# One fixed TensorE order from the inverse block to the first output tiles: attention as a generator of grouped steps

## The chip, the cores and the metric

One core of one Trainium2 chip runs the whole program. The metric is the device time of one execution in microseconds (us); before the change it is 1592.06 us, the median of 3 runs (1591.38 to 1592.39). PE is TensorE (matmuls), PEld its weight loads, DVE is VectorE, ACT is ScalarE, POOL is GpSimd, and SP is the engine that issues the DMA transfers.

## The reference

Two layers of a decoder trunk on a sequence of 512 tokens with 1024 channels, and a final norm. Cut to what matters here:

```python
n = RMSNorm(h);  p = n @ W_in                 # one input projection, split by columns
y_A = RWKV7_time_mix(p_A) @ W_oA              # 8 heads x 64, delta-rule state, group norm, gate
y_B = MLA(p_B) @ W_oB                         # 8 heads, causal softmax attention
h = h + (sigmoid(g_A) * y_A + sigmoid(g_B) * y_B) @ W_out
h = h + ConvFFN(RMSNorm(h))
...
# time mix, per token t and head
sa = state @ a_t
state = state * w_t + sa * b_t + v_t * k_t
y_t = state @ r_t
...
# attention, per block of 128 queries
s = (qn . kn + qr . kr) * scale;  s = where(causal, s, -1e30)
o = softmax(s) @ v
```

## The kernel before

**Products.** Activations lie with channels on the 128 partitions and the 512 tokens along the free axis. A weight product is done in split precision: `split` (L274) makes a high part `hi` on ACT and the remainder `lo` on DVE, and `mm3` (L245) does three matmuls of 128x512 per 128x128 weight block (L246 to L248). The weights stream from HBM in units of 512 KB (`raw`), which ACT and DVE split into `whi` (L201) and `wlo` (L202). `wtile` (L250) makes a tile of an output from 8 or 4 such blocks, and `Part` (L256) is the same piecemeal: `go(n)` does the next n blocks and, with the last, calls an end function.

**Order.** The program is written for a scheduler that puts every engine's instructions in an order of its own, by priority and readiness, except inside `manual_schedule`, where an engine keeps the order of the code. Every engine then works its queue strictly in that order, waiting on semaphores. Tiles come from pools with a number of buffers per tag: a tile that is asked for waits until the last reader of the one that had the buffer is done.

**A layer.** `mixer(l, ...)` (L425 to L962) begins with the input projection and the preparation of the time mix. Then, with TensorE in the order of the code (L647 to L815), come the triangular inverses of the chunks of 64 tokens, the rest of the projection (`parts4`: latents and gates), and the recurrence over 8 chunks c (L777 on): the state's read (L785), its sum xs (DVE, L789), the inverse applied (L795), a copy into Z (L798), the update's products with BT (L804), and the new state St (POOL and DVE, up to L815). Between these steps `filler()` puts two blocks of the gate products, six matmuls, as long as there are any left (`rest`).

What follows (L817 to L962) has no order of its own; the code comes as `outputs`, `norms`, `heads(0)`, `heads(1)`, `transposed`, `heads(2)`, `heads(3)` (L952), and the scheduler mixes it, and also pulls the products of the value tile Vt (L903) up into the recurrence:

- `chunk_out(i)` (L825): the chunk outputs into Z (copied by ACT, L844). `group_norm(i)` (L848) and `group_scale(i)` (L861): reductions on DVE, a square on ACT, a power (L858) and the scaling (L863) on POOL.
- `yop` (L867): four transposes of Z (L869) for a group p of 128 channels; loads of `bl` (L871) and `rg` (L873) from HBM, both with the tag "yl", which has two buffers; on DVE bl is scaled and summed (L874) and multiplied with rg (L875), then split, hi on ACT and lo on DVE (L279, L280). `transposed` does p = 0 and 1 in one PSUM tile xy, and then 2 and 3 in the next; there is one buffer for xy (two banks).
- `heads(p)` (L907), two heads at a time: the keys' products and K (ACT and POOL, L913), q (L921), and then, for each block b of 128 queries, a head at a time: scores `sc` of n = 128(b+1) keys (L929), the masked row minimum (DVE, L932), exp (ACT, L935), reciprocal (DVE, L936), scaling (ACT, L937), transposes of P into `pt` (L940; one bank), the copy PT (L942: on ACT for odd b, on DVE for even), and the value products into `po` (L947), of both heads into the two halves of the array. At the end po is split (L950).
- The output tiles of y_A: 8 times `wtile(yops)` (L957), four blocks each.

[...]

## Time and profile before

| what | us |
|---|---|
| median of 3 runs | 1592.06 |
| the profiled execution | 1593.16 |
| its span, first to last instruction | 1591.4 |
| TensorE busy | 1562.6 (98%) |
| DVE, ACT, POOL busy | 915.4, 661.5, 184.7 |
| inverse block to first output tile, layer 0 | 126.30 (227.60 to 353.90) |
| the same, layer 1 | 126.20 (1013.00 to 1139.20) |
| mean granted TensorE clock | 0.997 |

The span is 1.8 us shorter than the profiled execution's own time, which lies 1.1 us above the median. In the rows of a timeline the columns are the start, the duration, the engine, the line and operation, what it writes and reads, the shapes, and in brackets the idle time before it and what ended that. A row may hold several instructions of a kind (x4); a product in scores or values counts two records, a transpose or a matmul of a weight product one. A row of waits has the total, the number and the longest.

### The profile page before, as it was taken

The numbers are of one execution on the slowest core, as the hardware profiler recorded it, in microseconds if no ns is written. First come the engines' busy times: TensorE is split into PE (matmuls) and PEld (weight loads), VectorE is DVE, ScalarE is ACT, GpSimd is POOL, SyncE is SP. The second block draws the span as 40 slices with busy tenths as digits, with TensorE's granted clock in tenths as the row PEclk, the third lists the DMA queues.
The fourth block names the chain that finished last, engine by engine and source line by source line (L and its number), as shares of the span: only waits on it lengthen the run. The fifth ranks groups of instructions, "written<-read, shape, count | busy, mean of one in ns | idle before, by whom it ended". The sixth has DMA issues, their size and how long they took to land.

```text
span 1591.4 us, 22441 instructions
## 1 busy us (share of the span) xinstructions
PE 1562.6 (98%) x9052; PEld 1254.2 (79%) x9052; DVE 915.4 (58%) x1468; ACT 661.5 (42%) x996; POOL 184.7 (12%) x156
## 2 busy tenths in 40 slices
PE   8999999899999999999999999998999999999998
PEld 6878886668888888888878888775788888888887
DVE  6579786666555555533346668757564655554332
ACT  6445444563443333422244443446533434333222
POOL 1011102300311101100001111013002111010000
PEclk9999999999999999999999999999999999999999
DMA  5323322224423233233343233213253332332232
GB/s 192 125 100 132 121 81 67 88 74 147 123 96 99 93 97 102 93 108 120 110 146 106 94 106 120 74 48 101 86 162 103 97 102 93 95 104 93 93 104 82
DMA packets 57272, 166.08 MB, mean 104 GB/s; under 512 B 6352, under 2 KB 8528, under 8 KB 57168
## 3 DMA queue, kind: packets, MB, share of 16 engines
q1 hardware_dynamic: 57024, 164.48, 31.9%
q8 instruction: 71, 1.16, 0.3%
q14 instruction: 33, 0.27, 0.1%
q10 hardware_dynamic: 144, 0.16, 0.0%
HBM read 147.32 MB, written 17.30 MB: 103 GB/s over the span
## 4 chain that ended last, share of the span: by engine, by line
PE 91%; DVE 4%; issue 2%; ACT 1%; POOL 1%; DMA 0%; SPq 0%; POOLq 0%; DVEq 0%; ACTq 0%
PE acc L246 26%; PE acc L247 26%; PE acc L248 26%; PE sc L929 2%; PE po L947 2%; PE pt L940 1%; PE m L599 1%; PE xy L795 1%; DVE wlo L202 1%; PE m L607 1%; PE m L583 0%; PE xy L804 0%; PE m L524 0%; DVE X L661 0%; POOL mu L858 0%
## 5 line engine op out<-in xcount | busy, mean ns | idle before, releaser
L246 PE MATMUL acc<-hi,whi 128*128 128x512 f32 (+1 forms) x1910 | 752.4, 394 | 7.2 <-ACT hi L282 5.2
L248 PE MATMUL acc<-hi,wlo 128*128 128x512 f32 (+1 forms) x1910 | 742.6, 389 | 1.2 <-DVE wlo L202 1.2
L247 PE MATMUL acc<-lo,whi 128*128 128x512 f32 (+1 forms) x1910 | 742.8, 389 | 0.0
L201 ACT CAST whi<-raw 128x1024 fp32r<-128x1024 f32 (+2 forms) x249 | 253.5, 1019 | 547.2 <-PE acc L247 466.9
L246 PEld LDWEIGHTS acc<-hi,whi 128*128 128x128 f32 x1910 | 359.6, 188 | 82.5 <-ACT hi L282 5.2
L248 PEld LDWEIGHTS acc<-hi,wlo 128*128 128x128 f32 x1910 | 359.6, 188 | 76.1 <-DVE wlo L202 1.6
L247 PEld LDWEIGHTS acc<-lo,whi 128*128 128x128 f32 x1910 | 359.9, 188 | 72.4 <-issue 1.2
L202 DVE TENSOR_TENSOR wlo<-raw,whi 128x1024 fp32r<-128x1024 f32 (+2 forms) x249 | 309.5, 1244 | 175.9 <-ACT whi L201 175.5
L1027 POOL TENSOR_TENSOR c<-c,rstd 128x512 f32<-128x512 f32 x44 | 58.0, 1318 | 403.5 <-ACT c L1026 403.5
L1020 DVE TENSOR_TENSOR u<-acc,rstd 128x512 f32<-128x512 f32 x44 | 30.4, 692 | 104.7 <-PE acc L248 104.6
L1029 DVE TENSOR_TENSOR c<-c,acc 128x512 f32<-128x512 f32 x44 | 30.3, 688 | 86.4 <-POOL c L1027 86.4
L1026 ACT ACTIVATE c<-c 128x512 f32<-128x512 f32 x44 | 27.8, 632 | 81.6 <-DVE c L1025 81.6
L305 POOL TENSOR_TENSOR nv<-nv,cst 128x4 f32<-128x4 f32 (+1 forms) x10 | 10.0, 997 | 352.6 <-DVE nv L304 352.6
L341 POOL TENSOR_TENSOR nacc<-nacc,nsq 128x512 f32<-128x512 f32 x14 | 25.0, 1787 | 200.3 <-ACT nsq L340 200.3
L450 DVE TENSOR_TENSOR cur<-acc,rstd 128x512 f32<-128x512 f32 x28 | 19.1, 690 | 48.4 <-PE acc L248 39.3
L929 PE MATMUL sc<-K,q 128*128 128x128 f32 (+3 forms) x128 | 44.6, 446 | 1.1 <-DVE q L921 1.1
L935 ACT ACTIVATE P<-P,mn 128x128 f32<-128x128 f32 (+3 forms) x64 | 35.6, 556 | 17.2 <-issue 9.3
L932 DVE CUSTOM_DVE_ANT_0 P<-sc,cst 128x128 f32<-128x128 f32 (+3 forms) x64 | 30.7, 483 | 12.9 <-PE pt L940 10.4
L947 PE MATMUL po<-PT,Vt 128*64 128x128 f32 x320 | 37.5, 286 | 0.6 <-DVE PT L942 0.6
L937 ACT ACTIVATE P<-P,mn 128x128 f32<-128x128 f32 (+3 forms) x64 | 34.2, 557 | 6.6 <-DVE mn L936 6.6
L1023 ACT ACTIVATE c<-u,vec 128x512 f32<-128x512 f32 x44 | 35.7, 812 | 2.8 <-DVE u L1019 2.8
L947 PEld LDWEIGHTS po<-PT,Vt 128*64 128x64 f32 x320 | 22.3, 136 | 18.2 <-issue 7.3
(242 smaller groups left out, 1370.8 us busy)
## 6 DMA issues: line engine op xcount, KB each, us to landing
raw<-in_w SPq DMA_DIRECT2D x238, 512.0 KB, 3.4
gate_d<-gg SPq DMA_DIRECT2D x32, 256.0 KB, 2.1
AM<-gate_d SPq DMA_DIRECT2D x16, 256.0 KB, 5.9
gb<-gate_d SPq DMA_DIRECT2D x16, 256.0 KB, 3.6
h<-in_x SPq DMA_DIRECT2D x8, 256.0 KB, 4.6
rgate_d<-gt SPq DMA_DIRECT2D x8, 256.0 KB, 2.5
bl_d<-rk SPq DMA_DIRECT2D x8, 256.0 KB, 2.0
bl<-bl_d SPq DMA_DIRECT2D x8, 256.0 KB, 2.6
```

Of the source, the lines that this page charges most:

```text
L201: A.copy(hi, r)
L202: V.tensor_tensor(lo, r, hi.bitcast(F32), ALU.subtract)
L246: PE.matmul(ps, w[0], xx[0], start=first, stop=False)
L247: PE.matmul(ps, w[0], xx[1], start=False, stop=False)
L248: PE.matmul(ps, w[1], xx[0], start=False, stop=last)
L929: PE.matmul(sp[:, 0:n], qs[hh][:, 128 * b:128 * b + 128], ks[hh][:, 0:n], start=True, stop=True)
L932: V.tensor_tensor_reduce(out=P[:, 0:n], in0=sp[:, 0:n], in1=cst[:, C_CAUS + 512 - n:C_CAUS + 512], scale=-ATT_SCALE, scalar=1e30, op0=ALU. ...
L935: A.activation(P[:, 0:n], P[:, 0:n], AF.Exp, bias=mn[:, 0:1], scale=-1.0, accum_out=mn[:, 1:2])
L937: A.activation(P[:, 0:n], P[:, 0:n], AF.Copy, scale=mn[:, 2:3])
L947: PE.matmul(po[64 * hh:64 * hh + 64, 128 * b:128 * b + 128], Vt[:, kb, 64 * hd:64 * hd + 64], PTs[hh][:, 128 * kb:128 * kb + 128], start=k ...
L1023: A.activation(cc, u[:, 2:514], AF.Identity, bias=vc(l, "conv_b", i), scale=vc(l, "conv_w", 2 * FT + i))
L1027: G.tensor_tensor(cc, cc, rstd, ALU.mult)
```

## The change

TensorE's `manual_schedule` (an ExitStack `order`) now goes on from the inverse block through the recurrence, the attention, the chunk outputs, the transposes and the first four output tiles, so the order of all these on TensorE is that of the code; the other engines' order is still the scheduler's. Attention becomes a generator `attention(yops, ow)`: each `yield` ends a step of some matmuls, and `filler(n)` takes n steps of it wherever the recurrence and the chunk outputs leave room. A step t has the scores of both heads of one block, two or three pieces of `extra` (the next heads' projection, at the end the first output tiles), the transposes of the block before, head by head, and between them the value products of the block before that, both heads in pairs. The operations themselves are those of before.

Buffers: K and q together from 5 to 8, P and PT from 3 to 4 each, mn from 4 to 6. The gate parts' tile gg moves to a pool that lives longer (L711 after). The tags "yl" (2), sc, pt, po and xy are as before. A parameter of the program object, `dynamic_dma_scratch_size=1024`, is new. `heads`, `outputs`, `norms`, `transposed` and the old `filler` go.

```diff
+            order = ExitStack()
+            order.enter_context(tc.manual_schedule(engines={PE.engine}))
...
+                def attention(yops, ow):
+                    while parts4[7].i < 8:
+                        parts4[6 if parts4[6].i < 8 else 7].go(1)
+                        yield
...
+                            K = MT("K", "qk", 8)
...
+                    def turned(p, b, hh):
+                        n = 128 * (b + 1)
+                        pt = pb.tile([128, 512], F32, name="pt", tag="pt")
+                        for kb in range(b + 1):
+                            PE.transpose(pt[:, 128 * kb:128 * kb + 128], Ps[p, b][hh][:, 128 * kb:128 * kb + 128], ident)
+                        PT = MT("PT", "PT", 4)
+                        (A.copy if b % 2 else V.tensor_copy)(PT[:, 0:n], pt[:, 0:n])
+                        PTs.setdefault((p, b), []).append(PT)
...
+                    for t in range(18):
+                        if t < 16:
+                            p, b = steps[t]
+                            if b == 0:
+                                extra = project(p + 1) if p < 3 else ow()
+                            scores(p, b)
+                            yield
+                        for _ in range(2 if b < 3 else 3):
+                            if next(extra, 0) is None:
+                                yield
+                        if 0 < t < 17:
+                            turned(*steps[t - 1], 0)
+                        if t > 1:
+                            values(*steps[t - 2])
+                        if 0 < t < 17:
+                            yield
+                            turned(*steps[t - 1], 1)
+                        yield
...
                 for c in range(8):
...
-                        filler()
                         xs = tl.tile([128, 4, 2, 64], F32, name="xs", bufs=1)
...
+                        filler(2)
...
-                    filler()
                     V.tensor_copy(Z[ur:ur + 64, i, e, :].rearrange("p (q h i) -> p q h i", h=2, i=64),
                                   xy[ur:ur + 64, :, 256:512].rearrange("p h (q i) -> p q h i", i=64))
+                    filler(2)
...
-                        filler()
                         Sn = tl.tile([128, 4, 64], F32, name="St", tag="St", bufs=7)
...
+                        filler(1)
...
+                for i in range(4):
+                    chunk_out(i)
+                    filler(2)
+                grs = []
+                for i in range(4):
+                    grs.append(group_norm(i))
+                for i, gr in enumerate(grs):
+                    group_scale(i, gr)
+                filler(6)
+                for p in range(0, 4, 2):
+                    ps = xyt()
+                    yop(ps[:, 0, :], p)
+                    yop(ps[:, 1, :], p + 1)
+                    filler(2)
+                for _ in att:
+                    pass
+                while len(gas) < 4:
+                    firsts[len(gas)].go()
+                order.close()
+                for m in range(4, KT):
+                    ow_end(wtile(yops))
```

TensorE's order, first at two blocks of the attention in the middle of it, before (sc are scores, pt transposes of P, po value products, L246 to L248 weight products):

```order
L929 MATMUL sc<-K,q 128x384
L947 MATMUL po<-PT,Vt 64x128 x2
L940 MATMUL pt<-cst,P 128x128 x2
L247 MATMUL acc<-lo,whi 128x512
L929 MATMUL sc<-K,q 128x512
L940 MATMUL pt<-cst,P 128x128 x2
L947 MATMUL po<-PT,Vt 64x128
L929 MATMUL sc<-K,q 128x512
L947 MATMUL po<-PT,Vt 64x128 x3
L940 MATMUL pt<-cst,P 128x128 x3
```

The same on TensorE afterwards:

```order
L846 MATMUL pt<-cst,P 128x128 x2
L857 MATMUL po<-PT,Vt 64x128 x2
L846 MATMUL pt<-cst,P 128x128 x2
L828 MATMUL sc<-K,q 128x512 x2
L846 MATMUL pt<-cst,P 128x128 x3
L857 MATMUL po<-PT,Vt 64x128 x4
L846 MATMUL pt<-cst,P 128x128 x3
L828 MATMUL sc<-K,q 128x128 x2
```

The four value products of a block stood as one and three, with a score between; they stand together now, between the two heads' transposes of the next block, and the scores of both heads stand together.

TensorE at the transposes of Z (L869 before, L993 after). Before, each set of four (the first one's last row leads here) stood apart from the next:

```order
L869 MATMUL xy<-cst,Z 128x128
L929 MATMUL sc<-K,q 128x512 x2
L940 MATMUL pt<-cst,P 128x128 x2
L947 MATMUL po<-PT,Vt 64x128
L869 MATMUL xy<-cst,Z 128x128 x4
L947 MATMUL po<-PT,Vt 64x128 x3
L940 MATMUL pt<-cst,P 128x128 x6
L947 MATMUL po<-PT,Vt 64x128 x6
L940 MATMUL pt<-cst,P 128x128 x4
L246 MATMUL acc<-hi,whi 128x512
L247 MATMUL acc<-lo,whi 128x512
L869 MATMUL xy<-cst,Z 128x128 x4
```

Afterwards on TensorE:

```order
L846 MATMUL pt<-cst,P 128x128 x2
L993 MATMUL xy<-cst,Z 128x128 x8
L828 MATMUL sc<-K,q 128x512 x2
L846 MATMUL pt<-cst,P 128x128 x3
L857 MATMUL po<-PT,Vt 64x128 x4
L993 MATMUL xy<-cst,Z 128x128 x8
L846 MATMUL pt<-cst,P 128x128 x3
```

Two sets of four now follow each other, with one step of attention between the first two sets and the last two.

DVE at the same place (L874 and L998 read xy into bl, L875 and L999 multiply with rg, ISA is the masked minimum). Before, between the second bl's product and the third bl:

```order
L875 TENSOR_TENSOR bl<-bl,rg 128x512
L921 TENSOR_TENSOR q<-acc,rq 128x512
L932 ISA P,mn<-sc,cst 128x128
L932 ISA mn 128x1
L932 ISA P,mn<-sc,cst 128x128
L932 ISA mn 128x1
L280 TENSOR_TENSOR lo<-po,hi 128x512
L936 RECIPROCAL mn<-mn 128x1
L932 ISA P,mn<-sc,cst 128x256
L932 ISA mn 128x1
L874 SCALAR_TENSOR_TENSOR bl<-xy,vec,bl 128x512
```

Afterwards on DVE, from the second bl on:

```order
L998 SCALAR_TENSOR_TENSOR bl<-xy,vec,bl 128x512
L838 RECIPROCAL mn<-mn 128x1
L848 COPY PT<-pt 128x384
L999 TENSOR_TENSOR bl<-bl,rg 128x512
L838 RECIPROCAL mn<-mn 128x1
L998 SCALAR_TENSOR_TENSOR bl<-xy,vec,bl 128x512
L848 COPY PT<-pt 128x384
L834 ISA P,mn<-sc,cst 128x128
```

The second bl's product with rg and the third bl now follow each other with a reciprocal between, and the scores of the next block are reduced behind them.

## Prediction

> **What bounds the kernel now.** I read the page first, then the engines' busy time by stages, then TensorE's waits in the stage that the change touches, and last the timelines of that stage on each engine.

> ```profile
> span 1591.4 us, 22441 instructions
> ```

> The stretches below are the two stages that the change rewrites (from the inverse block to the first output tile, layer 0 and layer 1) and, between them, a stretch of plain weight products. The columns are the stretch, its length, the busy time of PE, PEld, DVE, ACT and POOL, the granted clock, the DMA share and GB/s.

> ```profile
> 227.60:353.90 126.30, 120.29 (x1328) 84.21 (x1328) 80.62 (x200) 72.25 (x158) 21.78 (x24) 1.00 0.24 75
> 400.00:1000.00 600.00, 598.83 (x2846) 491.13 (x2845) 327.40 (x440) 231.45 (x300) 69.61 (x51) 1.00 0.33 106
> 1013.00:1139.20 126.20, 119.68 (x1286) 83.37 (x1279) 79.85 (x200) 71.66 (x157) 21.79 (x24) 1.00 0.24 76
> ```

> TensorE bounds the kernel: outside these stages it stands for 1.2 us in 600. Inside them it shows 6.01 and 6.52 us idle, and no other engine is near its limit (DVE 64% of the stage, ACT 57%). So the order of the work can win two things only: TensorE's waits, and time in which it is busy at less than its rate. The waits of the first stage, by what ended them:

> ```profile
> PE xy L869 <- POOL Z L863: 1.2, 1, 1.2
> PE pt L940 <- DVE mn L936: 0.7, 1, 0.7
> PE xy L795 <- DVE xs L789: 0.7, 1, 0.7
> PE xy L833 <- ACT Z L844: 0.7, 2, 0.3
> PE xy L869 <- ACT Z L844: 0.6, 1, 0.6
> PE xy L785 <- DVE St L812: 0.6, 1, 0.6
> ```

> They are many and short; the longest is 1.2 us. What a wait really costs is more than the idle time shown, since the end of a matmul is modelled long. TensorE's timeline (start, duration, group) gives the factor:

> ```profile
> 309.07 0.55 PE L940 MATMUL pt<-cst,P 128*128 128x128 f32 x3
> 310.36 0.52 PE L940 MATMUL pt<-cst,P 128*128 128x128 f32 x3 [0.74 <-DVE mn L936]
> ...
> 312.33 0.66 PE L940 MATMUL pt<-cst,P 128*128 128x128 f32 x4
> 312.74 0.48 PE L246 MATMUL acc<-hi,whi 128*128 128x512 f32 x1
> ...
> 314.49 0.43 PE L947 MATMUL po<-PT,Vt 128*64 128x128 f32 x2
> 314.85 0.50 PE L246 MATMUL acc<-hi,whi 128*128 128x512 f32 x1
> 315.19 0.39 PE L247 MATMUL acc<-lo,whi 128*128 128x512 f32 x1
> 315.42 0.40 PE L248 MATMUL acc<-hi,wlo 128*128 128x512 f32 x1
> 315.75 1.09 PE L947 MATMUL po<-PT,Vt 128*64 128x128 f32 x14
> 316.76 0.71 PE L929 MATMUL sc<-K,q 128*128 128x128 f32 x4
> ```

> Four transposes that nothing holds up take 312.74 - 312.33 = 0.41, so the three at 309.07 could be followed at 309.38; the next start at 310.36. That is 0.98 lost where 0.74 is shown, 1.3 times. The stages therefore lose about 6.01 x 1.3 = 7.8 and 6.52 x 1.3 = 8.5 us, **8.15 a layer**.

> **What the change gives: grouping.** Every matmul of the stage is still done. But the value products of a block (two records each here) now stand together, both heads' in pairs, where before the first of them usually stood alone: the two records at 314.49 cost 314.85 - 314.49 = 0.36 and the fourteen at 315.75 cost 1.01. Seven products leave one half of the array empty once, so an eighth rides along free: the lone one's 0.36 is what grouping saves. By the instruction order 14 of a layer's 16 blocks are split so, and none afterwards: 14 x 0.36 = 5.0 us. Second, each visit to the half-array form slows its neighbours: the product at 314.85 takes 0.34 and the one at 315.42 takes 0.33, against 0.23 for the one between, so a visit costs 0.21 beside its own work. The order has 9 fewer visits a layer: 1.9 us. Grouping saves 5.0 + 1.9 = **6.9 a layer**, if nothing waits more than before.

> **What the change costs: waits.** If every stop went as well, the gain would be 15.05 a layer. So the question is how much TensorE stands in the new order, which it can't leave: before, whatever was ready stood at the front; now the next instruction is fixed.

> (a) The transposes of y. Before, the four sets of four stood far apart; now two and two, with one attention step between. The rows of before, on TensorE:

> ```profile
> 305.34 0.33 PE L869 MATMUL xy<-cst,Z 128*128 128x128 f32 x1
> 305.51 1.88 PE L929 MATMUL sc<-K,q 128*128 128x512 f32 x4
> 307.23 0.38 PE L940 MATMUL pt<-cst,P 128*128 128x128 f32 x2
> ...
> 307.90 0.66 PE L869 MATMUL xy<-cst,Z 128*128 128x128 f32 x4
> 308.49 0.65 PE L947 MATMUL po<-PT,Vt 128*64 128x128 f32 x6
> 309.07 0.55 PE L940 MATMUL pt<-cst,P 128*128 128x128 f32 x3
> ...
> 319.78 0.60 PE L869 MATMUL xy<-cst,Z 128*128 128x128 f32 x4
> ```

> What each set waits for is on DVE, ACT and the DMA queue. DVE:

> ```profile
> 305.75 0.75 DVE L874 SCALAR_TENSOR_TENSOR bl<-xy,vec,bl 128x512 f32<-128x512 f32 x1
> ...
> 306.53 0.69 DVE L875 TENSOR_TENSOR bl<-bl,rg 128x512 f32<-128x512 f32 x1
> ...
> 311.39 0.68 DVE L280 TENSOR_TENSOR lo<-bl,hi 128x512 fp32r<-128x512 f32 x1
> ...
> 314.71 0.69 DVE L875 TENSOR_TENSOR bl<-bl,rg 128x512 f32<-128x512 f32 x1 [1.32 <-DMA rg<-rgate_d]
> ```

> The loads, by time from issue to landing, and ACT, whose cast (L279) makes the high part:

> ```profile
> bl<-bl_d SPq DMA_DIRECT2D x8, 256.0 KB, 2.6
> rg<-rgate_d SPq DMA_DIRECT2D x8, 256.0 KB, 2.7
> ```
> ```profile
> 317.62 0.40 ACT L935 ACTIVATE P<-P,mn 128x128 f32<-128x128 f32 x1 [0.17 <-DVE mn L932]
> ...
> 318.02 0.60 ACT L279 CAST hi<-bl 128x512 fp32r<-128x512 f32 x1
> ...
> 320.24 0.80 ACT L937 ACTIVATE P<-P,mn 128x128 f32<-128x128 f32 x2
> ...
> 324.55 1.12 ACT L937 ACTIVATE P<-P,mn 128x384 f32<-128x384 f32 x2
> ```

> bl and rg have two buffers between them, and that is left as it was. So the second rg loads only when the first lo is done, and the third bl only when the second product with rg is. The last set shares its tile with the third and starts when DVE has read that one. From the end of the first set to the start of the fourth: 0.75 + 0.69 + 0.60 + 0.68 (first bl, product, hi, lo), 2.7 (rg lands), 0.69, 2.6 (bl lands), 0.75 = 9.5, and some 0.3 for seven handings-over (an estimate: 0.04 each, half of what lies between the modelled end of the transposes, 305.34 + 0.33, and DVE's read at 305.75): 9.8. TensorE has in that time two sets of transposes (0.41 to 0.59, from 307.90 to 308.49: 0.5 each), two scores of 512 (307.23 - 305.51 = 1.72), three transposes (0.4) and four value products (309.07 - 308.49 = 0.58) = 3.7. It stands for **6.1**: 0.8 before the second set, 0.9 before the third, which waits for the second bl, and 4.4 before the fourth. Before, the same chain took 319.78 - 305.34 = 14.4 with other work beneath and no stop, longer because lo came 4.2 us after its bl (311.39 against 307.22), behind softmax work on ACT and DVE. Were it 14.4 again, the stop would be 10.7; without the handings-over 5.8. I take 6.1, as hi and lo now directly follow their product on both queues.

> Queued behind those instructions are the copies of P's transposes (DVE) and the scaling of P (ACT), which TensorE wants next:

> (b) After the fourth set. ACT has two exp of 128 (0.40 each), hi of the second bl (0.60), two scales (0.80), two copies of K (0.60 each, as a 512-wide pass) and then the copy that frees the tile for transposed P (0.60), about 4.0 from when scores of 128 are reduced, 2 us into the stretch: 5.9. TensorE has two sets of transposes, two scores, six products of 0.23 to 0.34, four transposes and six value products, 4.3: a stop of 1.6. Then lo of the second bl, at 4.1, starts the buffer chain again: 2.7 + 0.69 + 0.60 + 0.68 + 2.7 + 0.69 + 0.60, and behind that last hi on ACT two scales of 384 (1.12) and a copy (0.40) = 14.3, where TensorE with its stop needs 11.7: a stop of 2.6. Together **4.2**; nothing, if ACT's and DVE's queues have run ahead while TensorE stood in (a).

> (c) The norms before the transposes. POOL carries the last part:

> ```profile
> 302.53 1.64 POOL L858 TENSOR_TENSOR mu<-mu,cst 128x8 f32<-128x8 f32 x1 [2.03 <-DVE mn L936]
> 304.24 1.04 POOL L863 TENSOR_TENSOR Z<-Z,mu 128x512 f32<-128x512 f32 x1
> ```

> For the last chunk: a copy (0.60), three DVE passes of 512 (0.69), a square on ACT (0.60), then 1.64 and 1.04 = 6.0, and DVE has among them a q, two P copies, two reductions of 384 and a lo, some 2.6, of which I count 2.1 on the path: 8.1. TensorE's cover after the chunk outputs is six products, three products, eight value products, two scores and six transposes, 5.2. Stop **2.9**; the ends are 1.2 (the shown wait on POOL alone) and 3.6.

> (d) The rest, inverse block and recurrence. The waits shown but for the two at L869 come to 6.0 - 1.8 = 4.2. Those on xs (0.7) and St (0.6) get products in front of them in every chunk and go: 2.9 x 1.3 = **3.8**. The state's cover falls from six products to three, 0.9 with the switch, against a wait of 0.6 x 1.3 = 0.8 where it had none: nothing, though it is thin. Ends: 2.5 (chunk outputs' 0.7 and one more go) and 5.5 (nothing goes).

> The larger buffers for K, q, P, PT and mn give the queues room to run ahead; they cost TensorE nothing, and with a fixed order they win only what (b) may lose.

> **The sum.** Stops 6.1 + 4.2 + 2.9 + 3.8 = 17.0 a layer against 8.15: +8.85. Grouping: -6.9. Net +1.95 a layer, +3.9 in two: span 1595.3. The profiled execution (1593.16, its span 1591.4) lies 1.1 above the median of the runs, 1592.06, so the forecast of the median is **1596.0**.

> **The rivals.** About 0.2%, 3.2 us, is what a measurement of this kernel can tell from no change. That is 1.6 a layer: with stops under 13.45 the change is faster, over 16.65 slower.

> Faster: while TensorE stands in (a), DVE and ACT finish all softmax work in hand, so (b) vanishes, (c) is the POOL wait of before (1.2) and (d) its low end. Stops 6.1 + 1.2 + 2.5 = 9.8; net -5.25 a layer: 1581.6. For it: DVE and ACT are idle for a third of the stage and more. Against it: the second chain in (b) is loads, which idle engines don't hasten. Chance 0.33. If all stops went, 1592.06 - 2 x 15.05 = 1562.0 would be the floor.

> No change: the stops total about 15 (half of (b) gone): 1592. Chance 0.25.

> Slower by the clock: both stages have clock 1.00, with no stop over 1.2 us; the new one of 4.4 is longer than any in them, so they can't say whether the clock holds behind it. If the 4.3 us of work up to the next stop ran at half rate, it would cost 4.3 more, of which the 1.6 of that stop is taken back: +2.7 a layer, 1601.4. Chance 0.07, on top of the forecast's stops. [...]

> **How the numbers follow.** The forecast (stops above 16.65 at full clock) has 0.35, and with the clock's 0.07 slower has 0.42; same 0.25; faster 0.33. With all upper ends (10.7 + 4.2 + 3.6 + 5.5 = 24.0) the net is +8.95 a layer, 1610; the range leaves out a tenth below the faster rival and less than a tenth at the top: 1579 to 1608.

> **What would show it.** Right: the four sets of transposes at L993 bunched within 10 us, waits of TensorE on DVE's bl near 6 us a layer (one over 4), a stage of some 128 us with about 15 us shown as waits at most, value products in groups of 4 to 16 records with none alone. Wrong: waits on bl under 3 us; or few waits behind them; or a stage under 123 us. [...]

## The result and the profile after

The changed kernel takes 1608.93 us (median of 4 runs, 1607.68 to 1609.35) against 1592.1 before: 1.0101 times, 95% interval 1.0089 to 1.0114. It is slower, as forecast, but by 16.8 us where 3.9 were forecast, and it lies 0.9 above the top of the range. The profiled execution has 1608.68 and this page (span, and the granted clock in 40 slices):

```profile
span 1606.9 us, 22378 instructions
...
PEclk9999999899999999999999999999999999999999
```

The clock row, all nines before, has an 8 in the slice of layer 0's attention. TensorE's largest waits in the whole program (total, times, longest):

```profile
PE pt L846 <- ACT PT L848: 11.5, 7, 3.3
PE xy L993 <- DVE bl L998: 9.4, 4, 3.8
PE acc L246 <- ACT hi L282: 5.2, 1, 5.2
PE xy L993 <- POOL Z L989: 3.7, 2, 1.9
PE pt L846 <- DVE PT L848: 3.7, 7, 0.9
PE sc L828 <- DVE q L818: 1.3, 2, 0.7
```

The recurrence's waits on xs and St are gone, and large ones stand at the transposes of y and at the bank of transposed P (the copies of PT). Without the 5.2 at the start of the program, which before has too, all shown waits add up to 33.3 us; before to 15.6. TensorE's timeline at the transposes of y in layer 0:

```profile
302.58 0.49 PE L993 MATMUL xy<-cst,Z 128*128 128x128 f32 x3
304.94 0.33 PE L993 MATMUL xy<-cst,Z 128*128 128x128 f32 x1 [1.87 <-POOL Z L989]
306.11 0.65 PE L993 MATMUL xy<-cst,Z 128*128 128x128 f32 x4 [0.84 <-DVE bl L998]
306.60 2.90 PE L828 MATMUL sc<-K,q 128*128 128x512 f32 x4
...
315.51 1.12 PE L993 MATMUL xy<-cst,Z 128*128 128x128 f32 x4 [3.83 <-DVE bl L998]
...
319.19 0.63 PE L246 MATMUL acc<-hi,whi 128*128 128x512 f32 x1
319.62 0.63 PE L247 MATMUL acc<-lo,whi 128*128 128x512 f32 x1
...
332.26 0.69 PE L846 MATMUL pt<-cst,P 128*128 128x128 f32 x2 [3.31 <-ACT PT L848]
```

The stops are there, and behind them something more: products start 0.43 apart (319.19, 319.62), not 0.23, and the two scores of 512 take 309.30 - 306.60 = 2.70, not 1.72. The chain behind the 3.83, on DVE (L999 is the product with rg) and on the DMA queue:

```profile
307.47 0.69 DVE L280 TENSOR_TENSOR lo<-bl,hi 128x512 fp32r<-128x512 f32 x1 [0.68 <-ACT hi L279]
...
311.35 0.68 DVE L999 TENSOR_TENSOR bl<-bl,rg 128x512 f32<-128x512 f32 x1
...
314.70 0.75 DVE L998 SCALAR_TENSOR_TENSOR bl<-xy,vec,bl 128x512 f32<-128x512 f32 x1 [2.60 <-DMA bl<-bl_d]
```
```profile
308.19 0.32 SPq L997 DMA_DIRECT2D rg<-rgate_d  x1
312.05 0.32 SPq L995 DMA_DIRECT2D bl<-bl_d  x1
```

The first lo ends at 308.16, and the second rg is issued at 308.19; the second product ends at 312.03, and the third bl is issued at 312.05. Both loads wait for their buffer, as the prediction had it.

```profile
303.91:307.32 3.41, 1.54 (x7) 1.02 (x8) 1.48 (x3) 1.43 (x3) 0.97 (x1) 1.00 0.00 0
307.32:310.73 3.41, 3.41 (x12) 1.67 (x12) 2.49 (x6) 1.38 (x4) 1.25 (x2) 0.50 0.54 154
310.73:314.15 3.42, 0.93 (x10) 0.48 (x6) 1.37 (x5) 1.72 (x4) 0.00 (x0) 1.00 0.27 74
314.15:317.56 3.41, 2.05 (x10) 2.06 (x11) 1.01 (x2) 0.00 (x0) 0.00 (x0) 0.50 0.01 3
317.56:320.97 3.41, 3.41 (x12) 2.72 (x12) 1.82 (x8) 2.84 (x9) 0.00 (x0) 0.50 0.00 0
320.97:324.39 3.42, 3.42 (x28) 2.80 (x27) 1.20 (x4) 2.09 (x5) 0.00 (x0) 1.00 0.27 77
```

A window in which TensorE is busy for 1.54 us (45%) is followed by one at 0.50, and so is one with 0.93 (27%). A window at half clock that is itself only 60% busy is followed by another. The emptiest two windows of this stage before, on the grid of that execution, were

```profile
295.50:298.91 3.41, 2.25 (x13) 1.45 (x12) 2.68 (x8) 3.05 (x6) 2.66 (x3) 1.00 0.11 40
298.91:302.32 3.41, 2.25 (x12) 1.45 (x10) 3.36 (x10) 1.88 (x7) 1.51 (x2) 1.00 0.00 0
```

with 66%, and the clock stayed. Layer 0 has three half-rate stretches after the change, layer 1 three. Half of TensorE's busy time in them is taken as what they cost: 7.3 + 4.9 = 12.2 us. Below, this is called the cost of the half clock; it is always that of one profiled execution. Before has one such stretch, from 22.43, outside these stages, which costs 1.7. The first stretch after the change follows a window that holds 1.03 us of the stop of 1.87 and the whole one of 0.84; the window from 298.91 before, with one stop of 1.16 in it, kept the clock. In these rows the drop goes with how much of a window TensorE works, 27% and 45% against 66%.

Grouping did what it was to do. The value products by line, before and after (busy us and mean ns, idle before):

```profile
L947 PE MATMUL po<-PT,Vt 128*64 128x128 f32 x320 | 37.5, 286 | 0.6 <-DVE PT L942 0.6
```
```profile
L857 PE MATMUL po<-PT,Vt 128*64 128x128 f32 x320 | 25.3, 289 | 0.0
```

The same 320 records keep TensorE busy 12.2 us less at the same length of each (286 and 289 ns), since they overlap more.

So between the two profiled executions: waits 33.3 - 15.6 = +17.7, clock 12.2 - 1.7 = +10.5, grouping -12.2, together +16.0; the spans differ by 15.5.

### The profile page after: what moved, and what is told of

Same layout as the page of the kernel before. It is cut to its first block, busy times and chain, and to the rows that moved or that the text cites. A ratio compares the mean times of both kernels' runs of the same rounds, so it can differ in the third digit from the quotient of the medians.

```text
span 1606.9 us, 22378 instructions
## 1 busy us (share of the span) xinstructions
PE 1559.8 (97%) x9052; PEld 1259.2 (78%) x9052; DVE 916.8 (57%) x1468; ACT 661.8 (41%) x996; POOL 188.7 (12%) x156
## 3 DMA queue, kind: packets, MB, share of 16 engines
q8 instruction: 71, 1.16, 0.3%
## 4 chain that ended last, share of the span: by engine, by line
PE 90%; DVE 5%; ACT 2%; POOL 2%; issue 1%; DMA 1%; POOLq 0%; DVEq 0%; SPq 0%; ACTq 0%
PE acc L246 26%; PE acc L247 26%; PE acc L248 26%; PE sc L828 2%; PE xy L928 1%; PE pt L846 1%; PE m L599 1%; POOL mu L984 1%; PE po L857 1%; PE m L607 1%; ACT whi L201 1%; POOL Z L989 1%; DVE wlo L202 1%; ACT P L837 1%; ACT P L839 0%
## 5 line engine op out<-in xcount | busy, mean ns | idle before, releaser
L246 PE MATMUL acc<-hi,whi 128*128 128x512 f32 (+1 forms) x1910 | 755.1, 395 | 6.3 <-ACT hi L282 5.2
L248 PE MATMUL acc<-hi,wlo 128*128 128x512 f32 (+1 forms) x1910 | 742.1, 389 | 0.6 <-DVE wlo L202 0.6
L247 PE MATMUL acc<-lo,whi 128*128 128x512 f32 (+1 forms) x1910 | 741.1, 388 | 0.0
L246 PEld LDWEIGHTS acc<-hi,whi 128*128 128x128 f32 x1910 | 359.6, 188 | 82.8 <-ACT hi L282 5.2
L248 PEld LDWEIGHTS acc<-hi,wlo 128*128 128x128 f32 x1910 | 359.5, 188 | 75.8 <-DVE wlo L202 1.0
L247 PEld LDWEIGHTS acc<-lo,whi 128*128 128x128 f32 x1910 | 359.8, 188 | 72.3 <-DVE lo L283 0.5
L846 PE MATMUL pt<-cst,P 128*128 128x128 f32 x160 | 32.0, 301 | 15.5 <-ACT PT L848 11.5
L846 PEld LDWEIGHTS pt<-cst,P 128*128 128x128 f32 x160 | 20.6, 151 | 28.4 <-ACT PT L848 14.5
## 6 DMA issues: line engine op xcount, KB each, us to landing
gate_d<-gg SPq DMA_DIRECT2D x32, 256.0 KB, 2.1
AM<-gate_d SPq DMA_DIRECT2D x16, 256.0 KB, 4.3
gb<-gate_d SPq DMA_DIRECT2D x16, 256.0 KB, 3.7
h<-in_x SPq DMA_DIRECT2D x8, 256.0 KB, 4.1
rgate_d<-gt SPq DMA_DIRECT2D x8, 256.0 KB, 2.7
bl_d<-rk SPq DMA_DIRECT2D x8, 256.0 KB, 2.0
bl<-bl_d SPq DMA_DIRECT2D x8, 256.0 KB, 2.6
```

The costliest lines, as they stand in the source:

```text
L246: PE.matmul(ps, w[0], xx[0], start=first, stop=False)
L247: PE.matmul(ps, w[0], xx[1], start=False, stop=False)
L248: PE.matmul(ps, w[1], xx[0], start=False, stop=last)
L846: PE.transpose(pt[:, 128 * kb:128 * kb + 128], Ps[p, b][hh][:, 128 * kb:128 * kb + 128], ident)
```

## The experiments

Theory A: the bunched transposes and the two buffers of bl and rg make the long stops, and the clock follows. Theory B: ACT, DVE and POOL can't keep up with the fixed order at all. Every kernel was timed together with the kernel before on the same chip; the medians of that were 1591.8 to 1592.8, and ratios are to it.

**e1, four buffers for bl and rg**, in short:

```diff
-bl/rg: tag="yl", bufs=2      P, PT: bufs=4
+bl/rg: tag="yl", bufs=4      P, PT: bufs=3
```

> The changed kernel with four buffers instead of two for bl and rg, paid for by one buffer each of P and PT. Theory A (the loads of bl and rg queue behind their own two buffers, and the long stops and the lower clock follow from that): TensorE's waits on bl fall from 9.4 us to under 3, those on the copies of transposed P from 15.2 to under 6, the clock holds (no half-rate stretch but at the ends of the run), time 1594 us, 1590 to 1598. Theory B (the fixed order itself: softmax and norms on ACT, DVE and POOL can't keep up with it, whatever the loads do): only the waits on bl go and others take their place, 1604 us or more.

1599.93 us (ratio 1.0049, 1.0034 to 1.0064). The loads' buffers cost 9 us, a little over half of the loss; but neither theory's number came. The waits changed place:

```profile
PE pt L846 <- DVE PT L848: 13.3, 14, 2.0
...
PE xy L993 <- DVE bl L998: 4.2, 4, 1.7
PE xy L993 <- POOL Z L989: 3.5, 2, 1.8
PE pt L846 <- ACT PT L848: 2.6, 4, 1.0
```

The half clock cost 9.7 us in this execution, 1.7 of it in a lone stretch elsewhere (from 1065.52).

**e2, products of no use in the stops** at the transposes (23 a layer, by `PE.matmul` of old operands into a spare acc tile).

> The changed kernel with 23 products more per layer whose result is not used, put where TensorE stands at the transposes of y (6 ahead of the first set, 3 ahead of the second and 14 ahead of the fourth, 5.4 us of work at 0.23 each). If the halved clock behind a stop is a large part of the loss (the slow stretches right behind these stops cost some 4 us in layer 0 and 2 to 3 in layer 1): clock whole there, 1602 us, 1600 to 1605, in spite of more work. If the stops alone are the loss: 1609 to 1612.

1604.9 us (1.0083, 1.0067 to 1.0098): 4.0 below the changed kernel in spite of more work. The half-rate stretches behind the transposes went, those behind the wait on ACT's copy (one a layer) stayed. This is in favour of the clock, but the waits changed too (13.4 on ACT's copies), so it proves little.

**e3, the first value product alone**, on e1:

```diff
+values(*steps[t - 2], 0)      # only kb = 0, hh = 0
 turned(*steps[t - 1], 0)
-values(*steps[t - 2])
+values(*steps[t - 2], 1)      # the others
```

> The kernel of the four load buffers, with the first value product of every block put ahead of the first head's transposes, so that it stands alone as most did before. If grouping is worth 0.36 us a block: 16 blocks in two layers, 11 us above the run with four load buffers, 7 at the least where some of it falls into stops. If it is worth nothing: within 2 us of that run.

1606.33 us (1.0090, 1.0075 to 1.0105), 6.4 above e1, under the 7 that was the least expected. The half clock cost 6.2 us in its profiled execution and 9.7 in e1's; with that, 9.9. e11 asks again without this muddle.

**e4, the kernel before with bl elsewhere:**

```diff
-bl = tb.tile([128, 512], F32, name="bl", tag="yl", bufs=2)
+bl = Z[:, p, 1, :]
```

> The kernel before, with bl loaded into a dead part of Z, so that rg has the two buffers for itself. Theory A says that the order before hid these loads: within 0.2% of before, 1589 to 1595 us. If the loads cost something there too: 1585 or less.

1593.55 us (1.0010, 1.0001 to 1.0020). The loads' buffers cost nothing in the order before.

**e5, the same line in the changed kernel.**

> The changed kernel with bl loaded into a dead part of Z, so that rg has the two buffers for itself and P, PT keep their four. If the loads' buffers are what the first test removed: like the run with four load buffers, 1600 us, 1597 to 1602. If the third buffer of P and PT that was given up there is what kept it slow (theory C): 1595 or less, with the waits on DVE's copies of transposed P back from 13.3 to 4 us.

1598.73 us (1.0033, 1.0020 to 1.0046): like e1, so theory C (the buffers of P and PT that e1 gave up) falls. The waits on DVE's copies went back to 3.6, but those on ACT's rose from 2.6 to 11.7.

**e6, work between the two heads' transposes**, on e5: one piece of `extra` before `turned(.., 0)`, the rest after the value products.

> The kernel with bl elsewhere, and in every step one or two pieces of the next projection moved from ahead of the first head's transposes to between the two heads' transposes. Theory D (the one bank for transposed P is copied out while TensorE has only the value products to do, 0.4 to 1.0 us, against a copy of 0.3 to 0.6 behind other work on its queue): waits on copies of transposed P under 5 us in two layers from 14 to 16, the clock mostly whole, 1588 us, 1584 to 1593. Theory B (ACT and DVE can't keep up with the order at all): the waits move to the scaled P or to the scores, 1598 or more.

1597.97 us (1.0038, 1.0024 to 1.0051). Theory D (the one bank for transposed P) falls: the waits on the copies are 15.6 in all, as in e5 (15.3), with the norms' and bl's 7.7 beside them.

**e7, the transposes of y apart**, on e6:

```diff
-filler(6)
+filler(8)
 for p in range(0, 4, 2):
     ps = xyt()
-    yop(ps[:, 0, :], p)
-    yop(ps[:, 1, :], p + 1)
-    filler(2)
+    for j in range(2):
+        yop(ps[:, j, :], p + j)
+        filler(3)
```

> As the kernel with work between the heads, and the transposes of y start two steps later, with three steps of attention behind each of the four sets. If what is left are the waits on the norms (POOL) and on bl: these, some 7 us in two layers, go under 2, and time is 5 to 8 us below the run with work between the heads; 1582 us if that one is 1588. If the work is only missing later: within 2 us of it.

1579.88 us (0.9919, 0.9904 to 0.9934): faster than both kernels, and 18.1 below e6, over twice what the waits at the transposes could give. Its waits:

```profile
PE acc L246 <- ACT hi L282: 5.5, 1, 5.5
PE pt L846 <- ACT PT L848: 4.9, 6, 1.0
PE pt L846 <- DVE PT L848: 3.1, 4, 1.1
PE sc L828 <- DVE q L818: 1.3, 2, 0.7
```

None is left at the transposes of y, those on the copies are halved, and no half-rate stretch is left before the end. Without the one at the start, all shown waits fell from e6's 27.2 to 13.3, and 4.9 of half clock went (1.7 of it a lone stretch elsewhere): 18.8, and the spans differ by 18.8.

**e8, e6's step alone**, without e5's line.

> The changed kernel with the work between the heads and nothing else; bl and rg share two buffers as there. If the loads' chain is a cost of its own: the wait on bl stays at 8 to 9 us with lower clock behind it, 1600 us, 1597 to 1604. If the one bank for transposed P was the root of all: 1592 or less.

1607.19 us (1.0086, 1.0069 to 1.0102). The wait on bl stayed at 9.3, with 10.1 of half clock, 3.4 of it in two lone stretches elsewhere. The time is 3 above the range of the first bound, but the one bank isn't the root.

**e9, e7's transposes alone** in the changed kernel.

> The changed kernel with nothing but the transposes of y moved: two steps of attention later, and three steps behind each of the four sets. bl and rg share two buffers, the steps are as in the changed kernel. If the bunched transposes are the root and the loads' chain only shows because of them: the waits at the transposes under 3 us, the clock whole, 1582 us, 1579 to 1587. If the two buffers or the heads' transposes cost by themselves: 1590 or more, with waits on bl or on copies of transposed P over 8 us.

1587.5 us (0.9969, 0.9957 to 0.9982): nothing but the place of sixteen transposes a layer takes 21.4 us off the changed kernel. Its waits:

```profile
PE pt L846 <- ACT PT L848: 9.4, 8, 1.5
PE acc L246 <- ACT hi L282: 5.7, 1, 5.7
PE pt L846 <- DVE PT L848: 3.8, 7, 0.9
PE xy L993 <- DVE bl L998: 2.9, 2, 1.6
PE pt L846 <- DVE mn L838: 2.5, 2, 1.3
```

Without the one at the start they add up to 22.9, 10.4 less than in the changed kernel, and the 12.2 of half clock are all gone: 22.6, and the spans differ by 22.7. Waits on bl are 2.9, on the copies 13.2, where e7 has none and 8.0. The time lies half a microsecond above the first bound: the bunching is the root, and buffers and steps cost a little by themselves.

**e10, e7 without the work between heads.**

> As e7, with the steps of the changed kernel (no work moved between the heads' transposes). If that work gave nothing of its own, as e6 beside e5 says: 1580 us, 1578 to 1583. If it was hidden in e6 behind the norms' wait: 1585 or more, with 6 us more of waits on copies of transposed P.

1583.23 us (0.9947, 0.9932 to 0.9962): 4.3 under e9 for the loads' buffers, 3.3 over e7 for the work between the heads, which gave 0.8 in e6, less than those runs scatter. Neither bound was met in time, but the waits on the copies are 15.2, 7 more than e7's, as the second had it: some of that work's gain had been hidden.

**e11, e7 with the first value product alone.**

> As e7, with the first value product of every block alone ahead of the first head's transposes. The clock is whole in e7, so this has the price of grouping without the clock's: 32 blocks by 0.36 = 11.5 us above e7, 1591 us (1588 to 1594), if a lone product costs what the trace of before showed; 1582 or less if it does not.

1592.55 us (1.0004, 0.9994 to 1.0013), 12.7 above e7. Its profiled execution has one half-rate stretch in layer 1, which costs 1.7 and which e7 has not; without it 11.0, or 0.34 a block, where 0.36 was expected. Grouping is worth about as much as all that e7 gains over before.

**e12, the copies by head:** `(A.copy if hh else V.tensor_copy)` instead of `b % 2`.

> As e7, with the copy of transposed P on DVE for the first head and on ACT for the second in every block, in place of DVE for even and ACT for odd blocks. If the 8 us of waits on these copies that e7 has left come from two copies of one block behind each other on one queue: they fall to 4, time 1576 us, 1573 to 1578. If from other work ahead on these queues: 1579 to 1582.

1579.71 us (0.9921, 0.9906 to 0.9936), the same as e7, as the second bound had it. The waits on the copies didn't fall: 11.2 on DVE's and 0.7 on ACT's, against 8.0 in all. So two copies behind each other on one queue aren't their cause; that it is other work on these queues isn't shown.

**The clock by itself.** e13 to e15 are e7 with one stop a layer made on purpose, and they differ only in what TensorE does in it. The chain of small operations on POOL holds up the third set of transposes:

```diff
 for p in range(0, 4, 2):
     ps = xyt()
+    if p:
+        scr = tb.tile([128, 256], F32, name="scr", bufs=1)
+        G.tensor_scalar(scr, Z[:, 1, 1, 0:256], 0.0, None, ALU.mult)
+        for _ in range(10):
+            G.tensor_tensor(scr, scr, scr, ALU.add)
+        G.tensor_tensor(Z[:, 0, 0, 256:384], Z[:, 0, 0, 256:384], scr[:, 0:128], ALU.add)
+        dummy(18)     # e14; 35 in e15; none in e13
```

> The kernel of e7, whose clock is whole, with one made stop a layer: a chain of 12 small operations on POOL (about 7 us) starts when the second product with rg is done and must end before the third set of transposes. The values stay the same. TensorE stands some 3 to 5 us a layer there. If only the stop counts: 6 to 10 us above e7, the time of the stops. If the clock halves behind a long stop: besides that a stretch of 3.41 or 6.83 us at half clock in each layer, so 3 to 6 us more than the stops shown.

1604.54 us (1.0076, 1.0063 to 1.0089). The stop came out longer than meant, 8.2 us a layer, and the time is 24.7 above e7: more than the stops' 16.4. The windows on the grid of its clock:

```profile
310.48:313.89 3.41, 0.04 (x1) 0.00 (x0) 0.73 (x1) 0.91 (x2) 3.09 (x5) 1.00 0.26 77
313.89:317.30 3.41, 0.00 (x0) 0.00 (x0) 0.00 (x0) 0.00 (x0) 3.02 (x6) 0.50 0.00 0
317.30:320.72 3.42, 2.00 (x9) 2.00 (x10) 0.81 (x2) 0.00 (x0) 1.21 (x3) 0.50 0.00 0
320.72:324.13 3.41, 3.41 (x11) 2.65 (x11) 1.99 (x7) 2.19 (x6) 0.00 (x0) 0.50 0.00 0
324.13:327.54 3.41, 3.41 (x28) 2.49 (x26) 3.19 (x8) 1.71 (x3) 0.00 (x0) 1.00 0.00 0
```

One full window of work at half rate follows the one in which work comes back: 11 records in 3.41 us, and 28 in the next.

> As e13, with 18 products whose result is not used (4.2 us at 0.23) put into the stop ahead of the third set. If the halved clock costs by itself: no half-rate stretch and 3 to 6 us less than e13, though it does more work. If the clock costs nothing here: e13's time or up to 2 us more.

1601.84 us (1.0062, 1.0045 to 1.0079), runs from 1597.66 to 1606.52. The products filled half of the stop, and 4.0 us stayed open; the runs scatter by 9 us, and the granted clock with them, from 0.997 in the fastest (1597.66) to 0.991 and 0.990 in the slowest two (1606.52 and 1605.93). As a test of the two bounds it is inconclusive.

> As e14 with 35 products of no use (8.2 us) in place of 18: e13 showed a stop of 8.2 us, and 18 left 4.0 of it open, so that whether the clock fell hung on where its windows lay. If the halved clock costs by itself: no half-rate stretch, and the stop's own 16.4 us in two layers over e7 but nothing more, 1596 us, 1594 to 1599, some 8 below e13 in spite of the work, and little scatter. If the clock costs nothing: e13's 1604 or more.

1596.47 us (1.0027, 1.0016 to 1.0037): 8.1 under e13 with 70 products more, and e7's 1579.9 plus the stops' 16.4. No wait on POOL is left, and by e13's records the half clock costs 8.4 us there. So the price of the clock is real, and half of the busy time in these stretches is about its size. It is no closer than a few us: e13 also shows 3.8 more of waits on the copies than e15, and e15's execution has a lone half-rate stretch of 1.7.

## Why the prediction was wrong

**Grouping, -6.9 a layer: right, a little large.** The value products' busy time fell by 6.1 a layer, and e11 gives 6.35 for the lone products, 5.5 without its half-rate stretch.

**(a), a stop of 6.1 from a chain of 9.8: the chain is right, the stop shorter.** The first set ends at 304.94 + 0.33 = 305.27 and the fourth starts at 315.51, 10.2 later. The waits on bl are 4.7 a layer, less than 6.1; the work in between took 10.2 - 4.7 = 5.5 and not 3.7, with one window of 3.41 us in it at half clock (1.7).

**(b), 4.2: right in kind, too small.** The first stop (1.6) doesn't show: at half rate the work in front of it, 4.3 in the prediction, took 322.06 - 315.51 = 6.55. The second is there, 3.31 against 2.6. ACT in front of it:

```profile
328.17 1.05 ACT L201 CAST whi<-raw 128x1024 fp32r<-128x1024 f32 x1 [1.18 <-PE acc L247]
...
330.33 0.60 ACT L279 CAST hi<-bl 128x512 fp32r<-128x512 f32 x1
330.84 1.11 ACT L839 ACTIVATE P<-P,mn 128x384 f32<-128x384 f32 x2
331.86 0.35 ACT L848 COPY PT<-pt 128x256 f32<-128x256 f32 x1
```

The last hi, the two scales and the copy follow each other as the prediction had them, but ACT works without a gap from 328.17 on. The split of a weight unit, which the prediction had not counted, and two exp hold the hi up until 330.33, where its product was done at 329.87; so the chain of loads and ACT's queue come out nearly together. All waits on the copies are (11.5 + 3.7) / 2 = 7.6 a layer.

**(c), 2.9: 1.9 shown** on POOL, between the lower end of 1.2 and the 2.9. **(d), 3.8: too large;** with q, T and Q only 1.2 a layer is shown, since the chunk outputs' waits went too.

The four together: waits rose by (33.3 - 15.6) / 2 = 8.85 a layer, just what the sum had, 17.0 - 8.15. That is luck in part: the errors of (b) and (d) cancel, and the 8.15 is the idle time of two stages times 1.3, where the 15.6 is that of the whole program as shown.

**The step that failed** is the clock, kept out of the sum and given a chance of 0.07: "both stages have clock 1.00, with no stop over 1.2 us; the new one of 4.4 is longer than any in them, so they can't say whether the clock holds behind it." Its price in the prediction, 2.7 a layer, was for one stretch of 4.3 us behind that one stop. There were three stretches a layer, of 3.41 to 6.83 us, also behind windows with several short stops and behind (b)'s; they cost 6.1 a layer, 12.2 us in all, and the forecast was 12.9 too low. Between the spans, 15.5 apart where 3.9 was forecast, the clock accounts for 10.5 and grouping, 12.2 where 13.8 were forecast, for 1.6: together 12.1, and the forecast of the difference was 11.6 too low. The condition was wrong too: the first stretch came behind stops of 1.87 and 0.84, with a window 45% busy, while e9 has none in these stages with stops of up to 1.6. And the chance of 0.07 rests on no row. In the changed kernel every window at full clock and busy for 45% or less, six in all, was followed by one at half; by that the forecast's own stop of 4.4 was enough: wherever the windows of 3.41 us lie, one of them has at least 2.2 us in that stop and is at most 36% busy.

**The rivals.** The faster one, that the queues run ahead in (a)'s stop so that (b) vanishes, failed: the second stop of (b) came, 3.31 long, as the prediction's own objection had it, and the half clock with it. "No change" asked for stops of about 15 a layer; 16.65 are shown, and without the clock that would be 17.7 - 12.2 = 5.5 us slower, a little over its 3.2. "Slower by the clock" named the cause, but priced it at 5.4 in two layers, where it cost 12.2.

That the order can gain, e7 shows: a fixed order with the same grouping, but the transposes apart, bl elsewhere and work between the heads, is 0.8% faster than before.

## What to carry to other kernels

A fixed order on the bounding engine pays for grouping, and a bunch of dependent steps in it can become a stop; follow each such bunch through the buffers of its loads and put other work between its parts. Count the stops per window of the clock as well as in sum: here a window of 3.41 us with TensorE busy for 45% or less cost up to 1.7 us more in the next. And when a stop looks cheap, time one on purpose, once empty and once filled with useless products: e13 and e15 differ by 8.1 us, and e13's records show 8.4 of half clock.

## What the runs showed of the hardware

In the traces before and after, the records of TensorE's clock stand at 1.00 or 0.50, and each stretch but the last, at the program's end, is 3.41 us long or a multiple of it: after, the stretches at half are four of 3.41 us and two of 6.83. Cut at that length from the clock's first record on (10.37), the kernel after has six windows at full clock with TensorE busy for 45% or less, and each was followed by one at half. Two of them (from 303.91 and 310.73) stand in the section on the result; the other four, each with the next window:

```profile
327.80:331.22 3.42, 1.15 (x9) 0.60 (x7) 3.40 (x10) 3.05 (x7) 0.00 (x0) 1.00 0.16 56
331.22:334.63 3.41, 2.37 (x5) 1.34 (x6) 1.18 (x2) 1.36 (x4) 0.00 (x0) 0.50 0.46 149
...
1095.80:1099.22 3.42, 1.10 (x6) 0.67 (x6) 1.30 (x5) 2.00 (x7) 2.58 (x2) 1.00 0.00 0
1099.22:1102.63 3.41, 2.94 (x7) 1.90 (x8) 1.92 (x5) 1.23 (x2) 0.00 (x0) 0.50 0.25 77
...
1106.04:1109.46 3.42, 0.00 (x0) 0.00 (x0) 0.80 (x2) 0.72 (x1) 0.00 (x0) 1.00 0.23 77
1109.46:1112.87 3.41, 3.37 (x14) 3.18 (x15) 1.23 (x6) 0.78 (x4) 0.00 (x0) 0.50 0.00 0
...
1123.11:1126.52 3.41, 0.38 (x3) 0.38 (x4) 3.17 (x8) 2.98 (x8) 0.00 (x0) 1.00 0.03 7
1126.52:1129.94 3.42, 3.42 (x7) 1.24 (x5) 0.70 (x2) 1.19 (x3) 0.00 (x0) 0.50 0.50 153
```

They are 34%, 32%, 0% and 11% busy. In the middle no share of its own decides: before, the windows from 295.50 and 298.91, 66% busy, kept the clock, and the one from 19.02, 65% busy (2.23 of 3.41 us), was followed by that execution's one half-rate stretch before the end, from 22.43. What sets these apart is not shown.

At half clock, the changed kernel's windows that were 60% and 69% busy (from 314.15 and 331.22) were followed by another at half, and the six busy for 86% or more by full clock. In e13 the one with 2.00 us (59%) was followed by another at half, and the one with 3.41 by full clock.

The windows lie differently in the two executions: counted from the first instruction, one begins at 298.91 before and at 303.91 - 3.41 = 300.50 after. That this is why e14, with 4.0 us of its stop left open, scatters from 1597.66 to 1606.52 is the author's estimate from these edges; no run tests it.
